# A hybrid attention and recurrence block: the opening stage rewritten around the second half of x

## The chip, the cores and the metric

The kernel runs on one core of a Trainium2 chip. The metric is the device time of one execution in microseconds (us), the median of several. The profile speaks of five engines: PE (TensorE, the matrix multiplications; PEld is its loading of the stationary operand), DVE (VectorE), ACT (ScalarE), POOL (GpSimd) and SP (SyncE, whose queue issues nearly all transfers of this kernel). Each engine works through its own queue in order.

## The reference

One layer of an encoder block on x of 1024 tokens by 1024 channels, all in float32:

```python
h = rms_norm(h_res, norm_w[layer])
z = jnp.einsum('bsd,dc->bsc', h, w_in[layer].astype(f32))
qkv_a, g_a, q_b, zf_fwd, zf_bwd, i_b, g_b, zgate_a, zgate_b = jnp.split(z, split_points, axis=-1)
...
merged = jax.nn.sigmoid(zgate_a) * y_a + jax.nn.sigmoid(zgate_b) * y_b
h_res = h_res + jnp.einsum('bsd,de->bse', merged, w_out[layer].astype(f32))
```

`rms_norm` divides each token's row by its root mean square and multiplies it by a weight per channel. Behind the one wide projection `z` come three groups of banded attention (8 heads of 64 each) and a gated linear recurrence in both directions. What matters here is only the start: the norm of x, and the first columns of `z`, which are the values V of the three attention groups (512 columns each).

## The kernel before, in words

**Numbers.** A float32 operand is split into a high part (a rounded type that PE takes at full speed, written by ACT) and a low part (what is left, a subtraction). Each product of two such operands is three matmuls: high by high, high by low, low by high. Weights are read in pages of 128x512 (`raw`), which become `whi` and `wlo`; x is normalised and split into `hh` and `hl` (in the code `hq[0]`, `hq[1]`, read through `hs`).

**Order.** The program is emitted by a planner. `Engine` and `Plan` (from line 46) keep a modelled clock for each engine; `Builder.tick` (line 251) puts a waiting task into its engine's queue once its inputs will be there within 1.4 us of PE's modelled clock. Each engine then runs its queue in order, and waits where the model was too early. Weight pages are split in order by such tasks after `b.auto()` (line 353), at most `RING` = 9 pages ahead of the last page that is freed; raw pages have 4 buffers. `run_unit` (line 484) runs one or several accumulation groups side by side over eight steps `kk`; a function `pre` may emit work ahead of each step. PSUM has two rings of tiles: `b.gps` with 3 and `b.bank` with 5. Finished groups are copied by ACT into one of 3 `stage` tiles and stored to DRAM through SP's queue.

**The opening** (lines 685 to 924). x comes transposed, `xT`, as 16 tiles of 128 channels x 512 tokens: half `k` = 0 holds tokens 64 to 575, half `k` = 1 tokens 576 to 1023 and 0 to 63.

1. The first half is multiplied by the norm's weights only (`prep_u`, line 710: `uhi` on ACT, `ulo` on DVE) and projected unnormalised into four PSUM tiles `ups` (loop at line 861), 8 x 4 x 3 = 96 matmuls. Beside it ACT squares x and DVE adds the squares into `acc`; the second half is squared in the loop's step 5 (`XB`). The low parts of the weights are made on POOL (`split`, line 358).
2. Within step 6 PE sums `acc` over the channels (`ss`, in `inv_rms`, line 722, for both halves at once), DVE makes the reciprocal root of the mean (`rsqrt`, line 553), and `spread` (line 731) turns it into a row on all partitions: DVE writes a diagonal `dg`, PE multiplies it with ones into `rB`.
3. The second half is normalised with `prep_h` (line 740: DVE x*w*rB, ACT `hh`, DVE `hl`), and `bias_tables` (line 772) writes the attention's bias tables to DRAM; each is then blown up there from DRAM to DRAM (`skewD<-tabD`).
4. Four groups of 128 tokens for V of attention group 0 run in two units: tokens 576 and 704, with `pre_b` normalising the second half step by step, then tokens 832 and the edge group (tokens 0 to 63 and 960 to 1023, whose operands POOL copies into `uhi`, `ulo` in `edge`). Meanwhile ACT scales the four `ups` with the reciprocal root into `stage` tiles (`scaled_v`), and the second unit's `pre_a` normalises the first half, which is loaded a second time through 4 buffers `x`.

**After it** (lines 926 to 992). V of attention groups 1 and 2: for each, six units of one group of 128 tokens and one unit of two, 8 x 24 matmuls. Beside them, for each of four blocks `c` of channels, `sums_h` on POOL and `sums_1`, `sums_2` on DVE form sums and differences of blocks of h, which `put_sum` splits (`S0h`, `S0l` ...). When all 16 are written (`blocks_start`), `run_quads` (line 432) starts with its products into `qA`: a scheme with 7 products for 8 in place of the plain projection. Then come attention, recurrence and output, which the change does not touch.

Of the kernel before, what the change touches and what calls it, by code (L numbers as in the profile page):

```python
# [18 lines left out]
S = 1024  # L19
# [10 lines left out]
LOWS = ("T2", "T4")  # L30
XR, SQ = 4, 2
XB = {5: (0, 1, 2, 3, 4, 5, 6, 7)}

# [177 lines left out]
class Builder:  # L211
# [145 lines left out]

    def split(self, raw, low="pool"):
        hi, lo = self.hir.get(), self.lor.get()
        scale = self.scales.get(self.split_next)  # L360
        if scale is None:
            self.p.act.activation(hi, raw, AF.Copy)
            getattr(self.p, low).tensor_tensor(lo, raw, hi.bitcast(F32), op=OP.subtract)
# [120 lines left out]
    def run_unit(self, unit):  # L484
# [87 lines left out]
def hybrid_block(ctx, tc, a, out):  # L572
# [114 lines left out]

    def load_x(k, d, new):
        xs[k, d] = new()
        s_.dma_start(xs[k, d], a["xT"][8 * k + d])  # L690

    def new_x():
        return pre.tile([128, 512], F32, tag="x", name=b.name("x"), bufs=XR)

    for d in range(4):
        load_x(0, d, new_x)
        b.feed()
    wp = bank("warm")
    for k in range(WARM):
# [10 lines left out]
    def prep_u(d):  # L710

        add = square(0, d - 1, xs[0, d - 1]) if d > 0 else None
        if d < 8:
            a_.activation(uhi[:, d], xs[0, d], AF.Copy, scale=nw[:, d:d + 1])
            v_.scalar_tensor_tensor(ulo[:, d], xs[0, d], nw[:, d:d + 1], uhi[:, d].bitcast(F32),
                                           op0=OP.mult, op1=OP.subtract)
        if d > 0:
            add()
            if d + XR - 1 < 8:
                load_x(0, d + XR - 1, new_x)  # L720

    def inv_rms():
        ps = b.gps.get(name="ss")
        for j in range(8):
            t_.matmul(ps[:, j:j + 1], acc[j // 4][:, 128 * (j % 4):128 * (j % 4) + 128], ones[:, 0:1],
                             start=True, stop=True)
        r = rsqrt(b, tiny, ps[:, 0:8], 8, 1.0 / D, "x")
        b.gps.done(ps)
        return r

    def spread(r):

        dg = pre.tile([128, 512], F32, tag="sq", name=b.name("dg"), bufs=SQ).rearrange("p (a t) -> p a t", a=4)
        v_.tensor_tensor(dg, ident[:, None, :].to_broadcast([128, 4, 128]),
                                r[:, :, None].to_broadcast([128, 4, 128]), op=OP.mult)
        ps = bank("rB")
        t_.matmul(ps, ones, dg, start=True, stop=True)
        return ps

    def prep_h(k, d, rB):  # L740

        parts = ((0, A0, 512 - A0), (512 - A0, 512, A0)) if k == 0 else ((0, A1, S - A1), (S - A1, 0, A0))
        if d < 8:
            x = xs[k, d]
            v_.scalar_tensor_tensor(x, x, nw[:, d:d + 1], rB, op0=OP.mult, op1=OP.mult)
            for c, t, n in parts:
                a_.activation(hs(0, d, t, n), x[:, c:c + n], AF.Copy)
        if d > 0:
# [14 lines left out]
    g_.memset(rb[32:33, :], NEG)  # L763
    oh = [stage.get() for _ in range(3)]

    def bias_rows():
        p = b.gps.get(name="tab")
        for g in range(3):
            t_.matmul(p[32 * g:32 * g + 8, 0:TABW], rb[:, 8 * g:8 * g + 8], oh[g][0:33, 0:TABW], start=True, stop=True)
        return p  # L770

    def bias_tables(p):
        g_.tensor_scalar(nqk[:, 0:3], nqk[:, 0:3], -0.125 / 128.0, None, op0=OP.mult)
        g_.tensor_scalar(nqk[:, 3:6], nqk[:, 3:6], -1.0 / 128.0, None, op0=OP.mult)
        for g in range(3):
            stage.done(oh[g])
            t = stage.get()
# [58 lines left out]

    def evac_v(g, t0, scale=None):
        def f(ps):
            t = stage.get()
            if scale is None:  # L840
                a_.activation(t, ps, AF.Copy)
                b.gps.done(ps)
            else:
                a_.activation(t, ps, AF.Copy, scale=scale)
            put[g] = put.get(g, 0) + 1
            if t0 < 0:
                def both():
                    s_.dma_start(vD[g, 0:64], t[0:64])
                    s_.dma_start(vD[g, S - 64:S], t[64:128])
                    stage.done(t)  # L850
                b.task("sp", [t], both, 1)
            else:
                store(vD[g, t0:t0 + 128], t)
        return f

    for d in range(LEAD):
        b.split_next_page()
        prep_u(d)
    ups = [bank("u") for _ in range(4)]
    rs = {}  # L860
    for d in range(8):
        wh, wl = b.w[d]
        for j in range(4):
            c = slice(128 * j, 128 * j + 128)
            for i, (l, r) in enumerate(((uhi[:, d, c], wh), (uhi[:, d, c], wl), (ulo[:, d, c], wh))):
                t_.matmul(ups[j], l, r, start=(d == 0 and i == 0), stop=(d == 7 and i == 2))
            if d == 6 and j == 1:
                r_ = inv_rms()
                for t in acc:
                    v_ring.done(t)  # L870
                for e in range(XR):
                    load_x(0, e, new_x)
        if d < 9 - LEAD:
            prep_u(d + LEAD)
            if d < 8 - LEAD:
                b.split_next_page()
        if d == 0:
            for e in range(8):
                load_x(1, e, v_ring.get)
            s_.dma_start(nqk, a["qk_w"])  # L880
            s_.dma_start(rb[0:32, :], a["rel_bias"])
            for g in range(3):
                s_.dma_start(oh[g][0:33, 0:TABW], a["c_onehot"][:, g])
        if d in XB:
            for e in XB[d]:
                square(1, e, xs[1, e])()
    rB = spread(r_[:, 4:8])
    groups = [tok_group(pos, t, evac_v(0, t), last=(t < 0 or t == 832),
                        first=(lambda d: (uhi[:, d, 0:128], ulo[:, d, 0:128])) if t < 0 else None)
              for t in (576, 704, 832, -64)]  # L890
    for d in range(2):
        prep_h(1, d, rB)
    bias_tables(bias_rows())
    b.auto()
    for j in range(4):
        b.task("act", [ups[j], r_], lambda j=j: scaled_v(j), 4, stage.soon, after=b.p.t["pe"] + 2.0 * j)

    def scaled_v(j):
        evac_v(0, 64 + 128 * j, r_[:, j:j + 1])(ups[j])

    def pre_b(kk):
        if kk < 7:
            prep_h(1, kk + 2, rB)
            edge(kk + 1)
        if kk == 0:
            edge(0)

    def edge(d):
        for e, u in enumerate((uhi, ulo)):
            for c, t in ((0, 0), (64, S - 64)):  # L910
                g_.tensor_copy(u[:, d, c:c + 64], hs(e, d, t, 64))

    def pre_a(kk):
        if kk == 0:
            rs["A"] = spread(r_[:, 0:4])
            prep_h(0, 0, rs["A"])
        prep_h(0, kk + 1, rs["A"])

    groups[0]["pre"] = pre_b
    groups[2]["pre"] = pre_a  # L920
    b.run_unit(groups[:2])
    b.run_unit(groups[2:])
    pos += 8
# [33 lines left out]
    def sums_2(c, x):  # L957
        v_.tensor_tensor(x[0, 1], x[0, 1], x[0, 0], op=OP.subtract)
        for k, t in ((0, x[1, 1]), (1, x[0, 0]), (2, x[2, 0]), (3, x[0, 1])):
            put_sum(k, c, t)  # L960

    for c in range(4):
        b.task("pool", [h[c2][:, c] for h in hq for c2 in h], lambda c=c: sums_h(c), 4, lambda: tmp.soon(5))

# [1071 lines left out]
```

## Time and profile before

| | us |
|---|---|
| median of 3 runs (1573.1 to 1578.47) | 1573.38 |
| the profiled execution's own time | 1571.46 |
| its span, from first to last instruction | 1569.7 |
| PE busy | 1517.6 |
| DVE busy | 960.9 |
| ACT busy | 807.4 |
| POOL busy | 481.3 |

The trace lists every instruction by its start and its duration. Matmuls overlap in the pipeline, so that a listed matmul of 0.39 us doesn't mean that the next starts 0.39 us later; the distance between starts is what counts. A name such as `gp<-whi,hh` gives the tile written and the tiles read (for PE the moving operand first). An entry in square brackets is the idle time ahead of an instruction and what ended it. PEclk is the share of full clock granted to PE. Nearly all instructions carry the line 56 of a helper, so tiles tell them apart.

### The profile page before, as it was taken

To read this page: it belongs to the slowest core of one execution; us is meant where nothing else is said; L and a number is where in the kernel's file an instruction comes from. 1 tells how busy PE (TensorE), PEld (TensorE's weight loads), DVE (VectorE), ACT (ScalarE), POOL (GpSimd) and SP (SyncE) were. 2 spreads that over 40 slices of the span, in tenths; PEclk is the share of its full clock that TensorE was granted. 3 is DMA by queue.
4 is the path that set the end of the run, shared out by engine and by line. 5 is a ranking of instruction groups with operands and counts; after the bars stand their busy time and mean duration, and the time that the engine had idled before them with its cause. 6 is when DMAs were issued, how large, how long until landed. Compare 5 with 4: busy or idle time off the path is not lost. (4 is left out here: it accounts for less than half of the span.)

```text
span 1569.7 us, 23099 instructions
## 1 busy us (share of the span) xinstructions
PE 1517.6 (97%) x8109; PEld 1238.1 (79%) x8109; DVE 960.9 (61%) x1891; ACT 807.4 (51%) x1693; POOL 481.3 (31%) x481
## 2 busy tenths in 40 slices
PE   8789999999999999999999999999999999999999
PEld 7578887778777787778777788878877878888887
DVE  6671487778878764544423438889788887643211
ACT  5523476666666655777642146565564642633210
POOL 3382333323333340020023254443243423003320
PEclk8999999999999999999999999999999999999999
DMA  7434433323425247465555651131211312842232
GB/s 220 138 104 131 132 101 120 119 71 118 116 56 141 67 141 245 148 193 152 151 149 157 208 165 41 48 101 41 86 50 41 103 40 74 307 123 94 87 122 93
DMA packets 171536, 188.15 MB, mean 120 GB/s; under 512 B 43297, under 2 KB 105884, under 8 KB 171420
## 3 DMA queue, kind: packets, MB, share of 16 engines
q1 hardware_dynamic: 163996, 186.23, 38.4%
q8 instruction: 64, 1.05, 0.3%
q10 hardware_dynamic: 7424, 0.45, 0.3%
q14 instruction: 52, 0.43, 0.1%
HBM read 130.69 MB, written 60.66 MB: 122 GB/s over the span
## 5 line engine op out<-in xcount | busy, mean ns | idle before, releaser
L56 POOL TENSOR_TENSOR wlo<-raw,whi 128x512 fp32r<-128x512 f32 x136 | 181.3, 1341 | 423.4 <-ACT whi L56 405.9
L56 POOL TENSOR_TENSOR wlo<-qraw,whi 128x512 fp32r<-128x512 f32 x100 | 137.4, 1380 | 296.3 <-ACT whi L56 266.8
L56 PE MATMUL gp<-whi,hh 128*128 128x512 f32 x344 | 142.4, 414 | 11.6 <-ACT hh L56 8.1
L56 ACT ACTIVATE whi<-raw 128x512 fp32r<-128x512 f32 x136 | 84.5, 626 | 111.0 <-PE gp L56 81.8
L56 PE MATMUL gp<-wlo,hh 128*128 128x512 f32 x344 | 137.7, 400 | 1.2 <-POOL wlo L56 1.1
L56 PE MATMUL gp<-hh,whi 128*128 128x512 f32 x336 | 137.9, 410 | 0.0
L56 PE MATMUL gp<-whi,hl 128*128 128x512 f32 x344 | 137.4, 399 | 0.5 <-DVE hl L56 0.5
L56 PE MATMUL gp<-hh,wlo 128*128 128x512 f32 x336 | 131.8, 392 | 0.0
L56 PE MATMUL gp<-hl,whi 128*128 128x512 f32 x336 | 131.4, 391 | 0.0
L56 ACT ACTIVATE whi<-qraw 128x512 fp32r<-128x512 f32 x140 | 85.9, 624 | 52.4 <-DVE qraw L56 35.2
L56 ACT ACTIVATE stage<-gp 128x512 f32<-128x512 f32 x60 | 35.3, 595 | 120.7 <-PE gp L56 103.1
L56 PEld LDWEIGHTS gp<-whi,hh 128*128 128x128 f32 x344 | 66.3, 193 | 34.4 <-ACT hh L56 9.3
L56 ACT ACTIVATE as<-as,neg 128x192 f32<-128x192 f32 (+2 forms) x192 | 83.7, 439 | 8.8 <-DVE neg L56 8.8
L56 DVE TENSOR_TENSOR qraw<-qraw,qraw 128x512 f32<-128x512 f32 x80 | 69.5, 870 | 29.0 <-POOL wlo L56 24.2
L56 PEld LDWEIGHTS gp<-whi,hl 128*128 128x128 f32 x344 | 66.4, 193 | 15.9 <-DVE hl L56 1.7
L56 PEld LDWEIGHTS gp<-wlo,hh 128*128 128x128 f32 x344 | 66.5, 193 | 15.6 <-POOL wlo L56 2.9
L56 DVE COPY apt<-pT 128x512 f32<-128x512 f32 (+2 forms) x50 | 29.0, 584 | 77.9 <-PE pT L56 77.9
L56 PE MATMUL gp<-sh,whi 128*128 128x512 f32 x192 | 74.7, 389 | 0.0
L56 PE MATMUL gp<-sl,whi 128*128 128x512 f32 x192 | 74.7, 389 | 0.0
L56 PE MATMUL gp<-sh,wlo 128*128 128x512 f32 x192 | 74.7, 389 | 0.0
L56 PEld LDWEIGHTS gp<-hh,wlo 128*128 128x128 f32 x336 | 63.4, 189 | 14.0
L56 PEld LDWEIGHTS gp<-hh,whi 128*128 128x128 f32 x336 | 63.7, 190 | 11.3
(255 smaller groups left out, 4042.9 us busy)
## 6 DMA issues: line engine op xcount, KB each, us to landing
raw<-in_w_in_dram SPq DMA_DIRECT2D x112, 256.0 KB, 2.8
qraw<-in_w_in_dram SPq DMA_DIRECT2D x80, 256.0 KB, 3.6
qkD<-ny SPq DMA_DIRECT2D x48, 256.0 KB
igD<-stage SPq DMA_DIRECT2D x32, 256.0 KB, 2.2
ig<-igD SPq DMA_DIRECT2D x32, 256.0 KB, 4.8
sgl<-sgD SPq DMA_DIRECT2D x32, 256.0 KB, 3.3
sgD<-stage SPq DMA_DIRECT2D x26, 256.0 KB, 2.2
ak<-qkD SPq DMA_DIRECT2D x6, 1024.0 KB, 7.3
```

The costliest lines, as they stand in the source:

```text
L56: got = f(*args, **kw)
```

## The change

- **Loads.** All eight tiles of the first half get tiles of their own, and are requested at the start: four beside the first weight pages, four right behind them. The second half is requested behind the first four splits instead of within the loop's step 0. The first half isn't loaded a second time. The one-hot matrix for the bias tables gets a tile of its own instead of the three `stage` tiles.
- **Low parts of the weights** are made on DVE instead of POOL while `b.low` is "dve", which is until the opening ends.
- **Squares.** The loop squares tiles 0 to 5 of the first half, then (in step 3) all eight of the second. PE's sum over channels is now for one half at a time: the second half's in step 7 of the loop, behind its first group. Tiles 6 and 7 of the first half are squared later, in steps 0 and 1 of the next unit, and its sum follows in step 3.
- **Unscaled products.** ACT copies the four `ups` unscaled into tiles `uv` (`keep_u`), scales them there when the root is known (`scaled_u`), and stores them from there.
- **One unit of four groups** (576, 704, 832 and the edge), the edge group in a `b.bank` tile. Its operands are read straight from the normalised x: POOL copies the high part, DVE subtracts.
- **The first half** is normalised by `pre_a` within the first three units of attention group 1 (one tile in three steps); these take the tokens in the order 640, 768, 896, and then 512, 0, 128 and so on. The last `prep_h(0, 8)`, which makes the low part of tile 7, is emitted twice.
- **Bias tables** are made behind the second of those units.
- **Sums.** `sums_h` runs on DVE instead of POOL, and each `put_sum` becomes a task of ACT of its own.

```diff
+    b.low = "dve"
     for d in range(4):
-        load_x(0, d, new_x)
+        load_x(0, d)
         b.feed()
+    for d in range(4, 8):
+        load_x(0, d)
...
     def prep_u(d):
-        add = square(0, d - 1, xs[0, d - 1]) if d > 0 else None
...
+        add = square(0, d - 1, xs[0, d - 1]) if 0 < d <= EA else None
...
-            if d == 6 and j == 1:
-                r_ = inv_rms()
...
+            if d == 7 and j == 0:
+                ss = b.gps.get(name="ss")
+                r1 = inv_rms(1, ss)
+                b.gps.done(ss)
...
+        if d == 3:
...
+            for e in range(8):
                 square(1, e, xs[1, e])()
...
+    rB = spread_out(spread(r1))
+    uv = [pre.tile([128, 512], F32, name=f"uv{j}") for j in range(4)]
+    groups = [tok_group(pos, t, evac_v(0, t), last=True) for t in (576, 704, 832)]
+    groups.append(tok_group(pos, -64, evac_v(0, -64, b.bank), last=True, first=lambda d: (uhi[:, d, 0:128], ulo[:, d, 0:128])))
+    groups[3]["ring"] = b.bank
...
+    def edge(d):
+
+        x = xs[1, d][:, 384:512]
+        g_.tensor_copy(uhi[:, d, 0:128], x)
+        v_.tensor_tensor(ulo[:, d, 0:128], x, uhi[:, d, 0:128].bitcast(F32), op=OP.subtract)
...
     def pre_b(kk):
+        if kk == 0:
+            edge(0)
         if kk < 7:
             prep_h(1, kk + 2, rB)
             edge(kk + 1)
...
+        if kk < 4:
+            keep_u(kk)
+        if EA + kk < 8:
+            square(0, EA + kk, xs[0, EA + kk])()
+        if kk == 8 - EA + 1:
+            rs["r"] = inv_rms(0, bank("ss"))
+            for j in range(4):
+                b.task("act", [rs["r"], uv[j]], lambda j=j: scaled_u(j), 4)
+
+        if kk == 5:
+            rs["dg"] = spread(rs["r"])
+        if kk == 7:
+            rs["A"] = spread_out(rs["dg"])
...
+    b.run_unit(groups)
...
+    def pre_a(kk):
+        if steps[0] % 3 == 0 and steps[0] < 27:
+            prep_h(0, steps[0] // 3, rs["A"])
+        steps[0] += 1
+
+    order = (5, 6, 7, 4, 0, 1, 2, 3)
+    grs = [tok_group(pos, 128 * i, evac_v(1, 128 * i), last=(k >= 6)) for k, i in enumerate(order)]
+    for k in range(3):
+        grs[k]["pre"] = pre_a
+        b.run_unit([grs[k]])
+        if k == 1:
+            bias_tables(bias_rows())
+    pre_a(0)
+    prep_h(0, 8, rs["A"])
...
     pctx.close()
+    b.low = "pool"
...
-            g_.tensor_tensor(x[t, k], hq[0][t, k][:, c].bitcast(F32), hq[1][t, k][:, c].bitcast(F32), op=OP.add)
+            v_.tensor_tensor(x[t, k], hq[0][t, k][:, c].bitcast(F32), hq[1][t, k][:, c].bitcast(F32), op=OP.add)
...
-            put_sum(k, c, t)
+            b.task("act", [t], lambda k=k, t=t: put_sum(k, c, t), 4)
```

More of the change, by code (lines that the diff above doesn't have):

```diff
@@ L30 @@
 LOWS = ("T2", "T4")
-XR, SQ = 4, 2
-XB = {5: (0, 1, 2, 3, 4, 5, 6, 7)}
+SQ, EA = 2, 6
 def _dram(ap, offset, dims):
@@ L217 @@
     eager = False
+    low = "pool"
     def __init__(self, ctx, tc, a):
@@ L356, in auto, with split @@
             self.offer(t, k)
-    def split(self, raw, low="pool"):
+    def split(self, raw, low=None):
         hi, lo = self.hir.get(), self.lor.get()
@@ L362, in split @@
             self.p.act.activation(hi, raw, AF.Copy)
-            getattr(self.p, low).tensor_tensor(lo, raw, hi.bitcast(F32), op=OP.subtract)
+            getattr(self.p, low or self.low).tensor_tensor(lo, raw, hi.bitcast(F32), op=OP.subtract)
         else:
@@ L686, in hybrid_block, with load_x @@
     xs = {}
-    def load_x(k, d, new):
-        xs[k, d] = new()
+    def load_x(k, d):
+        xs[k, d] = v_ring.get() if k else pre.tile([128, 512], F32, name=b.name("x"))
         s_.dma_start(xs[k, d], a["xT"][8 * k + d])
-    def new_x():
-        return pre.tile([128, 512], F32, tag="x", name=b.name("x"), bufs=XR)
+    b.low = "dve"
     for d in range(4):
-        load_x(0, d, new_x)
+        load_x(0, d)
         b.feed()
+    for d in range(4, 8):
+        load_x(0, d)
     wp = bank("warm")
@@ L710, in prep_u, with inv_rms @@
     def prep_u(d):
-        add = square(0, d - 1, xs[0, d - 1]) if d > 0 else None
[L713 to L717, printed above, removed]
-            add()
[L719 to L729, printed above, removed]
+        add = square(0, d - 1, xs[0, d - 1]) if 0 < d <= EA else None
+        a_.activation(uhi[:, d], xs[0, d], AF.Copy, scale=nw[:, d:d + 1])
+        v_.scalar_tensor_tensor(ulo[:, d], xs[0, d], nw[:, d:d + 1], uhi[:, d].bitcast(F32),
+                                       op0=OP.mult, op1=OP.subtract)
+        if add is not None:
+            add()
+    def inv_rms(k, ps):
+        for j in range(4):
+            t_.matmul(ps[:, j:j + 1], acc[k][:, 128 * j:128 * j + 128], ones[:, 0:1], start=True, stop=True)
+        return rsqrt(b, tiny, ps[:, 0:4], 4, 1.0 / D, "x")
     def spread(r):
@@ L735, in spread, with spread_out @@
                                 r[:, :, None].to_broadcast([128, 4, 128]), op=OP.mult)
+        return dg
+    def spread_out(dg):
         ps = bank("rB")
@@ L763, in hybrid_block @@
     g_.memset(rb[32:33, :], NEG)
-    oh = [stage.get() for _ in range(3)]
+    oh = pre.tile([33, 3, TABW], F32, name="oh")
     def bias_rows():
@@ L768, in bias_rows @@
         for g in range(3):
-            t_.matmul(p[32 * g:32 * g + 8, 0:TABW], rb[:, 8 * g:8 * g + 8], oh[g][0:33, 0:TABW], start=True, stop=True)
+            t_.matmul(p[32 * g:32 * g + 8, 0:TABW], rb[:, 8 * g:8 * g + 8], oh[:, g], start=True, stop=True)
         return p
@@ L775, in bias_tables @@
         for g in range(3):
-            stage.done(oh[g])
             t = stage.get()
@@ L835, in hybrid_block, with evac_v @@
     put = {}
-    def evac_v(g, t0, scale=None):
+    def evac_v(g, t0, ring=b.gps):
         def f(ps):
             t = stage.get()
[L840 to L844, printed above, removed]
+            a_.activation(t, ps, AF.Copy)
+            ring.done(ps)
             put[g] = put.get(g, 0) + 1
@@ L847, in both @@
                 def both():
-                    s_.dma_start(vD[g, 0:64], t[0:64])
-                    s_.dma_start(vD[g, S - 64:S], t[64:128])
+                    s_.dma_start(vD[g, S - 64:S], t[0:64])
+                    s_.dma_start(vD[g, 0:64], t[64:128])
                     stage.done(t)
@@ L858, in hybrid_block @@
         prep_u(d)
+    for e in range(8):
+        load_x(1, e)
     ups = [bank("u") for _ in range(4)]
-    rs = {}
     for d in range(8):
@@ L866, in hybrid_block @@
                 t_.matmul(ups[j], l, r, start=(d == 0 and i == 0), stop=(d == 7 and i == 2))
-            if d == 6 and j == 1:
-                r_ = inv_rms()
[L869 to L873, printed above, removed]
-            prep_u(d + LEAD)
[L875 to L879, printed above, removed]
+            if d == 7 and j == 0:
+                ss = b.gps.get(name="ss")
+                r1 = inv_rms(1, ss)
+                b.gps.done(ss)
@@ L880, in hybrid_block @@
+        if d + LEAD < 8:
+            b.split_next_page()
+            prep_u(d + LEAD)
+        if d == 3:
             s_.dma_start(nqk, a["qk_w"])
             s_.dma_start(rb[0:32, :], a["rel_bias"])
[L882 to L885, printed above, removed]
+            s_.dma_start(oh, a["c_onehot"])
+            for e in range(8):
                 square(1, e, xs[1, e])()
-    rB = spread(r_[:, 4:8])
@@ L888, in hybrid_block @@
-    groups = [tok_group(pos, t, evac_v(0, t), last=(t < 0 or t == 832),
-                        first=(lambda d: (uhi[:, d, 0:128], ulo[:, d, 0:128])) if t < 0 else None)
-              for t in (576, 704, 832, -64)]
+    rB = spread_out(spread(r1))
+    uv = [pre.tile([128, 512], F32, name=f"uv{j}") for j in range(4)]
+    groups = [tok_group(pos, t, evac_v(0, t), last=True) for t in (576, 704, 832)]
+    groups.append(tok_group(pos, -64, evac_v(0, -64, b.bank), last=True, first=lambda d: (uhi[:, d, 0:128], ulo[:, d, 0:128])))
@@ L891, in hybrid_block, with keep_u, scaled_u @@
+    groups[3]["ring"] = b.bank
+    b.auto()
     for d in range(2):
         prep_h(1, d, rB)
[L893 to L899, printed above, removed]
+    rs = {}
+    def keep_u(j):
+        a_.activation(uv[j], ups[j], AF.Copy)
+    def scaled_u(j):
+        a_.activation(uv[j], uv[j], AF.Copy, scale=rs["r"][:, j:j + 1])
+        b.task("sp", [uv[j]], lambda: (s_.dma_start(vD[0, 64 + 128 * j:192 + 128 * j], uv[j]), rs.__setitem__(j, 1)), 1)
@@ L904, in pre_b @@
             edge(kk + 1)
[L905 to L911, printed above, removed]
-    def pre_a(kk):
[L914 to L923, printed above, removed]
+        if kk < 4:
[4 more added lines that the diff above has]
+            rs["r"] = inv_rms(0, bank("ss"))
+            for j in range(4):
+                b.task("act", [rs["r"], uv[j]], lambda j=j: scaled_u(j), 4)
[3 more added lines that the diff above has]
+            rs["A"] = spread_out(rs["dg"])
+    groups[0]["pre"] = pre_b
+    keep_u(0)
+    keep_u = lambda j, f=keep_u: f(j) if j else None
+    b.run_unit(groups)
+    pos += 8
+    put[0] = 8
+    steps = [0]
+    def pre_a(kk):
+        if steps[0] % 3 == 0 and steps[0] < 27:
[10 more added lines that the diff above has]
+    prep_h(0, 8, rs["A"])
+    b.until(lambda: all(j in rs for j in range(4)))
     pctx.close()
+    b.low = "pool"
     gctx, sctx, tctx = ExitStack(), ExitStack(), ExitStack()
@@ L959, in sums_2 @@
         for k, t in ((0, x[1, 1]), (1, x[0, 0]), (2, x[2, 0]), (3, x[0, 1])):
-            put_sum(k, c, t)
+            b.task("act", [t], lambda k=k, t=t: put_sum(k, c, t), 4)
     for c in range(4):
-        b.task("pool", [h[c2][:, c] for h in hq for c2 in h], lambda c=c: sums_h(c), 4, lambda: tmp.soon(5))
+        b.task("dve", [h[c2][:, c] for h in hq for c2 in h], lambda c=c: sums_h(c), 4, lambda: tmp.soon(5))
     def blocks_start():
@@ L981, in blocks_start @@
         b.start_quads(blk["raw"])
-    for g, order in ((1, range(8)), (2, (4, 5, 6, 7, 0, 1, 2, 3))):
-        grs = [tok_group(pos, 128 * i, evac_v(g, 128 * i), last=(k >= 6)) for k, i in enumerate(order)]
+    for g in (1, 2):
+        if g == 2:
+            grs = [tok_group(pos, 128 * i, evac_v(g, 128 * i), last=(k >= 6))
+                   for k, i in enumerate((4, 5, 6, 7, 0, 1, 2, 3))]
         for k, gr in enumerate(grs[:6]):
+            if g == 1 and k < 3:
+                continue
             b.run_unit([gr])
```

6 lines of the change are left out of this document (1 added, 5 removed).

## Prediction, made before the changed kernel was run

> **What bounds the kernel now.** I read the page first, then the chain that ended last, the waits of PE up to 165 us, the stages by windows, and the timeline of the opening.
>
> ```profile
> span 1569.7 us, 23099 instructions
> ...
> PE 1517.6 (97%) x8109; PEld 1238.1 (79%) x8109; DVE 960.9 (61%) x1891; ACT 807.4 (51%) x1693; POOL 481.3 (31%) x481
> ```
> ```profile
> 1336.11 229.88 PE gp L56 x1014
> ```
> ```profile
> PE gp L56 <- ACT hh L56: 8.1, 2, 7.4
> PE ss L56 <- DVE v L56: 4.4, 1, 4.4
> PE gp L56 <- ACT stage L56: 2.8, 1, 2.8
> ```
> ```profile
> 6.50:25.10 18.60, 18.41 (x80) 14.41 (x79) 15.11 (x16) 13.93 (x25) 9.71 (x7) 1.00 0.88 288
> 25.10:41.20 16.10, 11.08 (x42) 8.16 (x42) 8.64 (x21) 4.34 (x8) 0.96 (x2) 0.68 0.40 127
> 171.10:1569.70 1398.60, 1365.73 (x7484) 1117.11 (x7482) 872.74 (x1765) 738.72 (x1563) 407.97 (x397) 1.00 0.38 116
> ```
>
> PE is busy for 97% of the span, and the chain of the end is PE work for its last 230 us. The windows give the length, then busy time (and instructions) of PE, PEld, DVE, ACT, POOL, then PE's granted clock, the DMA share and GB/s. Behind 171.10 PE is 98% busy at full clock; in 25.10 to 41.20 it is 69% busy at a clock of 0.68. So time that PE doesn't lose ahead of 171 us moves the end by as much. These are the borders of that stretch:
>
> ```profile
> 6.53 0.48 PE L56 MATMUL u<-whi,uhi 128*128 128x512 f32 x1
> ...
> 41.25 0.50 PE L56 MATMUL gp<-whi,hh 128*128 128x512 f32 x1 [0.70 <-ACT hh L56]
> ...
> 74.87 0.39 PE L56 MATMUL gp<-whi,hh 128*128 128x512 f32 x1
> ...
> 84.56 0.61 PE L56 MATMUL gp<-whi,hh 128*128 128x512 f32 x1
> ...
> 112.04 0.39 PE L56 MATMUL gp<-whi,hh 128*128 128x512 f32 x1
> ...
> 127.61 0.39 PE L56 MATMUL gp<-whi,hh 128*128 128x512 f32 x1
> ...
> 170.90 0.39 PE L56 MATMUL gp<-whi,hl 128*128 128x512 f32 x1
> ```
>
> These are the first `u` product and, counted through the timeline, numbers 1, 97, 121, 241, 289 and 480 of the `gp` products. From 127.61 to 170.90 lie 191 steps, 0.2266 us each: PE's dense pace. Against it the opening (96 products, 21.8 us) takes 34.7 and loses 12.9; the two units of V of group 0 (96) take 33.6 and lose 11.8; the first unit of group 1 (24) loses 4.3; the five after it (120) 0.3; the last pair (48) 4.7; group 2 nothing. Together 34.0 us: no more than this is to be had.
>
> **The opening part by part.**
>
> ```profile
> 7.55 0.63 ACT L56 ACTIVATE whi<-raw 128x512 fp32r<-128x512 f32 x1 [1.93 <-DMA raw<-in_w_in_dram]
> ...
> 21.26 0.68 DVE L56 TENSOR_TENSOR v<-v,sq 128x512 f32<-128x512 f32 x1
> 21.86 1.78 DVE L56 SCALAR_TENSOR_TENSOR ulo<-x,nw,uhi 128x512 fp32r<-128x512 f32 x1
> 23.57 6.89 DVE L56 TENSOR_TENSOR v<-v,sq 128x512 f32<-128x512 f32 x9
> 25.10 1.05 PE L56 MATMUL ss<-ones,v 128*128 128x1 f32 x8
> 30.52 1.86 PE L56 MATMUL ss<-ones,v 128*128 128x1 f32 x8 [4.36 <-DVE v L56]
> 32.42 0.17 DVE L56 TENSOR_SCALAR rv<-ss 128x8 f32<-128x8 f32 x1 [1.96 <-PE ss L56]
> 34.63 0.69 DVE L56 TENSOR_TENSOR dg<-ident,rr 128x512 f32<-128x512 f32 x1
> 38.78 1.02 PE L56 MATMUL rB<-dg,ones 128*128 128x512 f32 x2
> ...
> 39.73 0.82 PE L56 MATMUL tab<-stage,rb 33*8 33x384 f32 x6
> ```
>
> PE reached `ss` at 25.10 with 78 products done, 0.9 later than its pace gives from 6.53. With 87 ahead of it, it comes there at 27.1. When is the second half's sum ready? Loads go at 288 GB/s (first window), 0.91 us for 256 KB. The fourth was there by 7.55, so the thirteenth, weight page 4, which now follows four x tiles, comes at about 15.7; PE wants it at 18.3. From there DVE does low part, `ulo` and an addition for each of three pages and two operations for the last, 11 in all. They took 0.68 (21.26) and up to 1.78 (21.86) beside POOL's low parts. POOL makes none now, so I take 0.7: 7.7 us, to 24.0 with ACT's 0.6 ahead. Seven additions for the second half at 0.77 (6.89 for nine) end at 29.4. I take 28.8, a little less, since the window's mean rate holds the queue's gaps too; 27.1, no wait at all, is the lower bound. A wait of 1.7 remains of the 4.36. Then `ss` (four columns, 1.05), root (32.42 to 34.63, 2.2), `dg` 0.69 and hops of 0.4 put `rB` at 33.15; the last nine `u` products (2.0) fit into that, where before 18 of them at lowered clock held `rB` back from 35.3 to 38.78. From `rB` to the first `gp` 2.47 as before; the table's matmuls in that gap (39.73) were hidden by the wait on `hh`, and go. First `gp` at 35.6 in place of 41.25: **5.6 gained**; 7.3 are still lost.
>
> **The four groups.**
>
> ```profile
> 43.92 0.73 SPq L56 DMA_DIRECT2D skewD<-tabD  x1
> ...
> 45.87 2.40 SPq L56 DMA_DIRECT2D vD<-stage  x3
> ...
> 55.69 0.69 ACT L56 ACTIVATE stage<-u,rr 128x512 f32<-128x512 f32 x1 [8.08 <-DMA vD<-stage]
> ...
> 56.90 0.80 PE L56 MATMUL gp<-whi,hh 128*128 128x512 f32 x1 [7.45 <-ACT hh L56]
> ```
> ```profile
> L56 DVE TENSOR_TENSOR hl<-v,hh 128x448 fp32r<-128x448 f32 x8 | 5.9, 734 | 7.9 <-ACT hh L56 7.9
> L56 DVE SCALAR_TENSOR_TENSOR v<-v,nw,rB 128x512 f32<-128x512 f32 x8 | 5.8, 739 | 4.5 <-PE rB L56 4.5
> L56 DVE TENSOR_TENSOR hl<-v,hh 128x64 fp32r<-128x64 f32 x8 | 2.0, 244 | 0.0
> ```
>
> Here the fourth scaled copy waited for a `stage` tile whose store sat behind the blown-up table: 45.87 to 55.69. ACT runs in order, so `hh` stood behind it, and PE behind `hh`: 7.45. The copies into `uv` need no such tile and the table comes later, so this wait goes. What is late next is DVE. Over the unit it does eight times 0.74 + 0.73 + 0.24 for the second half, eight low parts at 0.68, eight `edge` subtractions (128x128, not in the trace: between 0.24 for 64 columns and 0.73 for 448; 0.3), two additions, the root and `dg`: 13.7 + 5.4 + 2.4 + 1.4 + 2.9 = 25.8, less the overlap of neighbouring operations (rows start 0.67 apart). PE has 21.8 + 1.05 (`ss`) + 1.02 (`rA`) = 23.9. They nearly tie; I give PE 1.0 for the first two steps, where DVE starts with it. POOL's copies, ACT's `uv` copies and squares run ahead and cost nothing unless DVE's queue stops for them; if it did, each is under 0.7. The wait of `rsqrt` on `ss` in step 3 holds DVE for 2.2 us, and behind it stands the `hl` of step 5, two steps off, so PE feels nothing.
>
> ```profile
> 26.00:27.00 1.00, 0.15 (x2) 1.00 0.32 61
> 27.00:28.00 1.00, 0.00 (x0) 0.50 0.88 305
> 33.00:34.00 1.00, 1.00 (x4) 0.50 0.11 41
> ```
>
> Clock (after the busy time of PE): PE stopped at 26.15 and the clock halved at 27.0, with only one-column `ss` products in the two us before. At 33 four products fit in a us. The changed kernel has three gaps of 1.2 to 1.7 us within 9 us, with `ss` and `rB` between; one lowered stretch while PE has work (some 4 us at half pace) costs 2.0, and none or two are the bounds, 0 and 4. The Trainium skill, "TensorE: Matmul & The Clock Gate", Part 1, has the clock fall after an idle window of about 3.4 us; by that rule no gap here is long enough, and the sum would be 2.0 less. The row speaks against it, since PE had been idle for under 1 us.
>
> So the unit takes 23.9 + 1.0 + 2.0 = 26.9 for 21.8: 5.1 lost instead of 11.8, **6.7 gained**, and ends at 62.5.
>
> **Groups 1 and 2.**
>
> ```profile
> 79.79 0.50 PE L56 MATMUL gp<-wlo,hh 128*128 128x512 f32 x1 [0.86 <-POOL wlo L56]
> ...
> 113.47 0.63 ACT L56 ACTIVATE S1h<-xs 128x512 fp32r<-128x512 f32 x1 [2.77 <-DVE xs L56]
> ...
> 115.67 0.75 PE L56 MATMUL gp<-whi,hh 128*128 128x512 f32 x1 [2.79 <-ACT stage L56]
> ...
> 122.16 0.69 DVE L56 TENSOR_TENSOR S3l<-xs,S3h 128x512 fp32r<-128x512 f32 x1
> ```
>
> In the first unit of group 1, PE ate pages faster than POOL made low parts. Pages 8 to 15 now become free to split one per step of the four-group unit (2.7 us, against DVE's 0.7), so all are ready: **4.3 gained**. In the pair, PE waited for an evacuation that stood on ACT behind `S1h`, which waited for DVE. With `put_sum` a task of its own, and DVE alone on the sums (48 operations at 0.69, 33 us), this mostly goes. Bounds for it are 0 and the old 4.7; I keep 1.5, nearer to none since an evacuation has two units (10.9 us) to spare. The table's matmuls (0.82) now stand on PE's path and are added. Normalising the first half (1.7 a tile, three steps or 2.0 us each) hides under PE; the doubled `hl`, 1.0, does too. Gain here 4.3 + 0.3 + 4.7 - 1.5 - 0.8 = **7.0**.
>
> **Sum:** 5.6 + 6.7 + 7.0 = 19.3. The profiled execution took 1571.5 (1.8 around its span), so 1552.2; the median of the runs lies 1.9 above that execution, so **1554.1**, said as 1554.
>
> **The rivals.**
>
> *DVE sets the opening's pace.* For it: 25.8 against 23.9 in the unit, and a sum of squares that may come 0.6 later. Against: operations start closer than they last. Price 1.9 + 0.6, and a second lowered clock stretch 2.0: 4.5, so 1558.6.
>
> *The store wait comes back in groups 1 and 2.* The tables now fall into units that also store through three `stage` tiles. For it: 9.8 us behind one table. Against: a tile comes round after three units, 16.3 us. It decides if two tables follow within 16 us. Price 7.45 and 2.0 of clock: 1563.5.
>
> *Slower: the sums hold up the products of* `qA`. Those need all 16 parts, ready at 122.85 before, with 48 us to spare. On DVE the 48 operations at 1.78 (beside POOL's low parts) take 85.4 us; they start at 79.6 (62.5, three units, 0.8), so end at 165. Loads, a split and a low part follow, which took the opening 6.5 from nothing to its first product: `qA` at 171.5, and 2.0 of clock, where before it followed the last `gp` at 171.1. That is 2.4 slower: 1575.8. It decides from DVE's end at 162.6 on. The Trainium skill, "SBUF — State Buffer", Who interferes with whom, has DVE operations with two SBUF inputs shut out for the whole of a POOL read; by that rule each can pay. Only some 8 low parts fall into this stretch, so I hold it unlikely.
>
> *No effect:* the start of `qA` hangs on something that doesn't move, a transfer for instance. Nothing in the waits names one: 1573.
>
> **How the numbers follow.** About 0.5% (7.9 us) is what a measurement of this kernel can tell from none. Chances: forecast 0.60, DVE 0.20, store wait 0.12, no effect 0.05, slower 0.03. All of the first three lie below 1565.5, but the third nearly at it: faster 0.90; same 0.08; slower 0.02, the far end of the last. The range takes the forecast's bounds (clock 2.0, pair 1.5, squares 1.4 less: 1549; one more for pages and hops) and the first two rivals up to the store wait: 1548 to 1564.
>
> **What would show it.** In the profile after: `ss` waits under 3 us on DVE's `v`; first `gp` near 35.6; no wait of ACT on `vD<-stage` ahead of the unit's end at 62.5; no PE wait on `wlo` in group 1; none on `stage` over 1.5; `qA` from 152. Wrong if the first `gp` comes after 39, if ACT waits on a store in groups 1 and 2, or if `qA` starts after 160.

## The result, and the profile after

| | before | after |
|---|---|---|
| median of 4 runs each, us | 1575.47 (1573.1 to 1578.47) | 1551.97 (1546.83 to 1554.76) |
| the profiled execution's own time | 1571.46 | 1546.83 |
| its span | 1569.7 | 1545.0 |

The ratio of after to before is 0.9846, with a 95% interval of 0.9812 to 0.988: 1.5% faster, 23.5 us. The forecast was 1554 within 1548 to 1564.

The page of the changed kernel, its waits of PE up to 165 us, and its stages by windows (length, busy time and instructions of PE, PEld, DVE, ACT, POOL, then granted clock, DMA share, GB/s):

```profile
span 1545.0 us, 23058 instructions
...
PE 1508.1 (98%) x8109; PEld 1232.0 (80%) x8109; DVE 966.8 (63%) x1945; ACT 809.7 (52%) x1697; POOL 435.4 (28%) x424
```
```profile
PE gp L55 <- ACT hh L55: 1.4, 1, 1.4
PE warm L55 <- DVE warm L55: 1.4, 1, 1.4
PE gp L55 <- DVE hl L55: 1.2, 1, 1.2
PE rB L55 <- DVE dg L55: 0.9, 1, 0.9
PE ss L55 <- DVE v L55: 0.3, 1, 0.3
```
```profile
33.60:59.70 26.10, 24.69 (x106) 19.01 (x107) 20.49 (x53) 16.51 (x36) 4.71 (x9) 1.00 0.35 113
59.70:104.20 44.50, 44.50 (x199) 36.07 (x198) 39.35 (x64) 22.19 (x47) 7.52 (x5) 1.00 0.42 142
104.20:147.70 43.50, 43.50 (x193) 36.02 (x192) 14.82 (x18) 13.12 (x22) 10.43 (x8) 1.00 0.37 115
147.70:1545.00 1397.30, 1365.84 (x7484) 1117.39 (x7483) 869.43 (x1765) 738.77 (x1563) 411.89 (x397) 1.00 0.38 117
```

No wait of PE in this stretch is longer than 1.45 us; before there was one of 7.4, one of 4.4 and one of 2.8. PE has as many instructions as before (8109). From 59.70 on it is busy throughout, in the stage in which DVE now has the most to do (39.35 of 44.50). Behind `qA` the two kernels need nearly the same: 1397.3 here from 147.70, 1398.6 before from 171.10. So the gain lies in front of `qA`, at the borders that the prediction used (timeline of the changed kernel):

```profile
6.07 0.48 PE L55 MATMUL u<-whi,uhi 128*128 128x512 f32 x1
...
27.03 1.02 PE L55 MATMUL ss<-ones,v 128*128 128x1 f32 x8 [0.27 <-DVE v L55]
...
31.10 1.10 PE L55 MATMUL rB<-dg,ones 128*128 128x512 f32 x2 [0.89 <-DVE dg L55]
...
33.65 0.50 PE L55 MATMUL gp<-whi,hh 128*128 128x512 f32 x1 [1.45 <-ACT hh L55]
...
59.73 0.39 PE L55 MATMUL gp<-whi,hh 128*128 128x512 f32 x1
...
65.17 0.39 PE L55 MATMUL gp<-whi,hh 128*128 128x512 f32 x1
...
104.23 0.39 PE L55 MATMUL gp<-whi,hh 128*128 128x512 f32 x1
...
147.75 0.39 PE L55 MATMUL qA<-hh,whi 128*128 128x512 f32 x1
```

The first `u` is 0.5 us earlier than before; the opening up to the first `gp` takes 27.6 in place of 34.7, the four groups 26.1 in place of 33.6, the first unit of group 1 5.4 in place of 9.7, the rest of group 1 39.1 in place of 43.1, group 2 its 43.5 as before. Together `qA` starts 23.4 us earlier (171.13 before).

### The profile page after: what moved, and what is told of

Read it like the earlier page. It is cut to its first block, busy times and chain, and to the rows that moved or that the text cites. A ratio compares the mean times of both kernels' runs of the same rounds, so it can differ in the third digit from the quotient of the medians.

```text
span 1545.0 us, 23058 instructions
## 1 busy us (share of the span) xinstructions
PE 1508.1 (98%) x8109; PEld 1232.0 (80%) x8109; DVE 966.8 (63%) x1945; ACT 809.7 (52%) x1697; POOL 435.4 (28%) x424
## 5 line engine op out<-in xcount | busy, mean ns | idle before, releaser
L55 POOL TENSOR_TENSOR wlo<-raw,whi 128x512 fp32r<-128x512 f32 x119 | 161.3, 1361 | 437.1 <-ACT whi L55 424.1
L55 POOL TENSOR_TENSOR wlo<-qraw,whi 128x512 fp32r<-128x512 f32 x100 | 141.2, 1420 | 289.7 <-ACT whi L55 260.6
L55 PEld LDWEIGHTS gp<-hh,whi 128*128 128x128 f32 x336 | 63.7, 190 | 11.3
```

Source lines behind the costliest of these rows:

```text
L55: got = f(*args, **kw)
```

## The experiments

The total of one kernel varies by 3 to 14 us between runs, so parts of a few us can't be told apart by it. The borders in the trace are sharper: in the six other runs that leave the opening as changed, the first `gp` came 26.7 to 28.2 us after the first `u`, in the changed kernel 27.6. But each border comes from one profile, so a difference under 1.5 us at a border isn't shown by it alone. Each experiment has both, in us. `gp` 97 is the first product of attention group 1, 121 that of its second unit, 289 that of group 2. Each ratio is to runs of the kernel before that were taken beside it (their medians lie between 1572.26 and 1575.47), so ratios compare better than medians:

| kernel | first `u` | first `gp` | `gp` 97 | `gp` 121 | `gp` 289 | `qA` | median | ratio to before, 95% |
|---|---|---|---|---|---|---|---|---|
| before | 6.53 | 41.25 | 74.87 | 84.56 | 127.61 | 171.13 | | |
| after | 6.07 | 33.65 | 59.73 | 65.17 | 104.23 | 147.75 | 1551.97 | 0.9846 (0.9812, 0.9880) |
| after, once more | 6.55 | 34.02 | 61.20 | 66.64 | 105.70 | 149.22 | 1549.87 | 0.9848 (0.9824, 0.9873) |
| before, late table | 6.54 | 41.18 | 67.72 | 75.48 | 113.59 | 164.11 | 1564.83 | 0.9938 (0.9917, 0.9958) |
| before, new sums | 6.55 | 40.88 | 74.80 | 86.08 | 125.43 | 168.95 | 1572.94 | 0.9999 (0.9981, 1.0017) |
| before, both | 6.32 | 40.72 | 67.62 | 76.59 | 114.71 | 158.23 | 1560.99 | 0.9920 (0.9903, 0.9937) |
| after, old sums | 5.68 | 33.52 | 59.60 | 65.04 | 109.14 | 162.44 | 1562.60 | 0.9937 (0.9909, 0.9965) |
| after, sums on POOL | 6.01 | 34.24 | 60.32 | 65.76 | 109.79 | 161.36 | 1563.42 | 0.9930 (0.9906, 0.9955) |
| after, `put_sum` direct | 6.02 | 33.34 | 59.46 | 64.90 | 103.96 | 148.50 | 1552.22 | 0.9859 (0.9833, 0.9884) |
| after, two units | 6.38 | 33.06 | 64.15 | 69.59 | 108.65 | 152.17 | 1554.27 | 0.9867 (0.9833, 0.9900) |
| after, low parts on POOL | 6.20 | 35.30 | 60.82 | 66.26 | 105.32 | 148.84 | 1554.53 | 0.9870 (0.9837, 0.9904) |
| after, all squares first | 6.55 | 34.45 | 60.92 | 66.36 | 105.42 | 148.94 | 1551.65 | 0.9859 (0.9838, 0.9880) |
| after, late root | 6.19 | 33.44 | 59.82 | 65.71 | 104.77 | 148.29 | 1551.81 | 0.9861 (0.9837, 0.9884) |
| after, late root and filled gaps | 5.66 | 32.99 | 58.43 | 64.32 | 103.38 | 146.90 | 1548.33 | 0.9843 (0.9824, 0.9861) |

**The late table, alone.** In the kernel before, the bias tables move behind the second unit.

```diff
-    oh = [stage.get() for _ in range(3)]
+    oh = pre.tile([33, 3, TABW], F32, name="oh")
...
-    bias_tables(bias_rows())
     b.auto()
...
     b.run_unit(groups[2:])
+    bias_tables(bias_rows())
```

> The kernel before with one part of the change alone: the bias tables are made behind the second unit of group 0 (their one-hot matrix in a tile of its own). Theory (the store wait behind the blown-up table costs 7.45 us of PE and 2.0 of clock behind it): 7 to 9.5 us less than before, ratio 0.994 to 0.9955, and no wait of ACT on vD<-stage ahead of 63 us. Rival (the wait is only the last of several that end together, and DVE or the pages take its place): under 3 us less, ratio above 0.998.

The ratio is 0.9938, 9.5 us, the upper end of what the theory gave; in the profile the two units of group 0 gain 7.1 (26.5 for 33.6). The trace shows more. Up to product 289, where group 2 starts, the gain is 14.0 us. The pair, too, loses nothing now (10.9 from 102.71 to 113.59), though the sums are as before. But 7.0 of the 14.0 are lost in group 2, which had lost nothing before:

```profile
116.60 0.50 PE L56 MATMUL gp<-whi,hh 128*128 128x512 f32 x1 [1.49 <-ACT whi L56]
...
118.11 0.50 PE L56 MATMUL gp<-wlo,hh 128*128 128x512 f32 x1 [1.00 <-POOL wlo L56]
...
119.79 0.80 PE L56 MATMUL gp<-wlo,hh 128*128 128x512 f32 x1 [0.72 <-POOL wlo L56]
```

PE now comes to group 2's pages before ACT and POOL have made them.

**The sums as before, in the changed kernel.**

```diff
-            v_.tensor_tensor(x[t, k], hq[0][t, k][:, c].bitcast(F32), hq[1][t, k][:, c].bitcast(F32), op=OP.add)
+            g_.tensor_tensor(x[t, k], hq[0][t, k][:, c].bitcast(F32), hq[1][t, k][:, c].bitcast(F32), op=OP.add)
...
-            b.task("act", [t], lambda k=k, t=t: put_sum(k, c, t), 4)
+            put_sum(k, c, t)
...
-        b.task("dve", [h[c2][:, c] for h in hq for c2 in h], lambda c=c: sums_h(c), 4, lambda: tmp.soon(5))
+        b.task("pool", [h[c2][:, c] for h in hq for c2 in h], lambda c=c: sums_h(c), 4, lambda: tmp.soon(5))
```

> The changed kernel with the sums as before: sums_h on POOL, put_sum called directly. Theory (the pair of group 1 lost 4.7 us because its evacuation stood behind put_sum on ACT): 3 to 5 us more than the changed kernel, so some 18 us less than before (0.9885), with a PE wait on ACT stage of 2 to 3 us in the pair. Rival (the sums start some 7 us earlier now, and an evacuation has 10.9 us to spare, so their form costs nothing): within 1 us of the changed kernel, 0.986.

`qA` starts 14.7 us later than in the changed kernel, where I expected 3 to 5, and the ratio is 0.9937 for the changed kernel's 0.9846 and 0.9848. The timeline of the pair and of group 2's start, with what stopped each engine:

```profile
95.26 0.63 ACT L55 ACTIVATE S1h<-xs 128x512 fp32r<-128x512 f32 x1 [1.80 <-DVE xs L55]
...
96.83 0.57 ACT L55 ACTIVATE stage<-gp 128x512 f32<-128x512 f32 x1
...
97.46 0.80 PE L55 MATMUL gp<-whi,hh 128*128 128x512 f32 x1 [3.40 <-ACT stage L55]
```
```profile
111.90 0.50 PE L55 MATMUL gp<-wlo,hh 128*128 128x512 f32 x1 [1.70 <-POOL wlo L55]
...
114.11 0.63 ACT L55 ACTIVATE S1h<-xs 128x512 fp32r<-128x512 f32 x1 [2.72 <-DVE xs L55]
116.35 0.79 PE L55 MATMUL gp<-whi,hh 128*128 128x512 f32 x1 [1.87 <-ACT whi L55]
```
```profile
109.10:162.40 53.30, 48.28 (x193) 37.53 (x193) 13.73 (x14) 15.34 (x26) 17.64 (x13) 0.90 0.33 104
```

The pair loses its 5.0 as expected (104.23 less 93.35 there, 109.14 less 93.22 here). Group 2 loses 9.8 more: its low parts and its high parts stand on POOL and on ACT behind the sums, and with these waits the clock is 0.90 on the mean of the stage, the last row.

**Which half of that change?** Two runs, each with one half of the diff above: the sums on POOL with `put_sum` still a task of its own, and the sums on DVE with `put_sum` called directly.

> The changed kernel with sums_h on POOL again, but each put_sum still a task of its own. Theory (two separate causes: POOL's sums stand ahead of group 2's low parts, which cost 9.8 us at group 2's start, and put_sum called directly stands ahead of the pair's evacuation, 5.0 us): waits on wlo at the start of group 2 stay, the pair's wait goes, and qA starts near 157.5. Rival (both come from ACT standing behind put_sum): qA near 148.

> The changed kernel with put_sum called directly as before, but sums_h on DVE. By the theory of two causes: the pair's wait on ACT stage comes back with up to 5.0 us, no wait on wlo, qA between 150 and 153. Rival (the direct call costs something only where DVE waits for POOL's sums): qA at 147.8 to 148.5.

The theory of two causes fell. With POOL's sums the pair's wait came back in spite of the tasks (3.4), and group 2 lost 8.0, most of the 9.8 with the old sums; `qA` at 161.36. With the direct call alone `qA` starts at 148.50, 0.75 later, and group 2 takes 44.5 for 43.5, with one wait of 0.71 on POOL's `wlo`. So it is the engine for all but some 1 us. The groups of the stage show how, first of the changed kernel, then with the old sums (count, busy time, mean ns):

```profile
L55 DVE TENSOR_TENSOR xs<-xs,xs 128x512 f32<-128x512 f32 x16 | 11.8, 755 | 0.3
L55 DVE TENSOR_TENSOR xs<-hh,hl 128x512 f32<-128x512 f32 x16 | 14.4, 959 | 0.1
```
```profile
L55 DVE TENSOR_TENSOR xs<-xs,xs 128x512 f32<-128x512 f32 x16 | 21.1, 1340 | 4.7 <-POOL xs L55 4.1
L55 POOL TENSOR_TENSOR xs<-hh,hl 128x512 f32<-128x512 f32 x16 | 25.3, 1608 | 30.3 <-DVE hl L55 22.3 <-DVE S0l L55 6.7 <-DVE S2l L55 0.6
```

Sixteen additions take 14.4 us on DVE and 25.3 on POOL, and beside POOL DVE's own take 1340 ns in place of 755. A likely link, read from the code and not tested: the planner sets DVE's 512 columns down at 0.61 us and POOL's at 1.24, so it thought the sums done sooner than they were, and put `S1h` ahead of the evacuation and of the pages in ACT's queue, as a task or not.

**The new sums in the kernel before, and both parts in it.**

> The kernel before with the change of the sums alone: sums_h on DVE, each put_sum a task of its own. The last two runs put the whole cost on POOL's sums. Then here only the pair of group 1 gains, since its group 2 loses nothing: 4.7 us, qA at 166.4, ratio 0.997. Rival (DVE has no room for 16 more operations, or the wait in the pair has another cause): qA at 171 or later.

> The kernel before with two parts: late bias tables and the new sums. The late tables alone brought 14.0 us up to the first product of group 2 and kept 7.0 of them at qA, with waits on wlo in between. Theory (the other 7.0 went back because POOL's sums came ahead of group 2's low parts): no wait on wlo, qA near 157, ratio 0.991. Rival (POOL's low parts themselves are too slow there): qA stays near 164.

Alone the sums bring nothing that can be measured in the total (0.9999, interval 0.9981 to 1.0017, where I expected 0.997), and `qA` at 168.95 lies between the theory's 166.4 and the rival's 171. The pair's 4.7 are gained (10.9 from 114.55 to 125.43), but the first unit of group 1 loses 1.6 (11.3 for 9.7), where POOL's low parts now run beside DVE's sums (five in 8.35 us from 78.34 on, in 6.21 before), and 1.0 goes in the units after it. With the late table together, group 2 has no wait on `wlo` any more (43.5 from 114.71 to 158.23) and `qA` starts at 158.23: 12.9 of the 23.4 us. The 7.0 that the late table had to give back are kept.

**Two units in place of one.**

```diff
-    groups = [tok_group(pos, t, evac_v(0, t), last=True) for t in (576, 704, 832)]
+    groups = [tok_group(pos, t, evac_v(0, t), last=(t == 832)) for t in (576, 704, 832)]
...
-    b.run_unit(groups)
+    b.run_unit(groups[:2])
+    b.run_unit(groups[2:])
```

> The changed kernel with the four groups in two units of two, as before. Theory (DVE needs about 2.4 us a step for the second half whatever PE does, and only four groups side by side give PE as much): the first unit runs at DVE's pace, some 20 us for 10.9 of PE work, the second at PE's, so 7 to 9 us more than the changed kernel, some 14 us less than before (0.991). Rival (the gain comes from the moved table and squares alone, and the number of units doesn't matter): within 1.5 us of the changed kernel, 0.986.

The first unit took 20.2 us (33.06 to 53.27) and the second 10.9: 31.1 for 26.1. The 20 us are the theory's number, but not by DVE's pace alone: PE waited for DVE 3.2 us in the first unit (0.38, 0.74 and 2.03), and the clock fell twice in it, to 0.83 on the mean:

```profile
33.00:53.20 20.20, 16.99 (x58) 12.19 (x59) 16.00 (x46) 11.52 (x28) 4.71 (x9) 0.83 0.19 65
```

`qA` comes 4.4 later than in the changed kernel, with that lowered clock in it: less than the 7 to 9 expected, where I had left out what the single unit itself loses (26.1 for 21.8). The totals don't tell the two apart (0.9867, interval 0.9833 to 0.9900).

**The low parts on POOL again**, without the line `b.low = "dve"`.

> The changed kernel with the weights' low parts of the opening on POOL again. Theory (a DVE operation beside a POOL low part takes 1.78 in place of 0.7 us, and the sum of squares and the four-group unit hang on DVE): the second half's squares end 3 to 5 us later and PE waits for them, 3 to 7 us more than the changed kernel, 0.988 to 0.9905. Rival (DVE sheds 17 operations of 0.69 us, which outweighs the slower ones): equal or up to 2 us less than the changed kernel, 0.985.

PE waited 1.54 for the squares (0.27 in the changed kernel), and the first `gp` came 1.65 later; by `qA` 1.1 of it was left. The direction at the first `gp` is the theory's, the size at most half of it. At `qA` nothing is shown: the unaltered kernel's second profile below starts it later still (149.22), and the ratio, 0.9870, is not told apart either.

**All squares of the first half first.**

```diff
-SQ, EA = 2, 6
+SQ, EA = 2, 8
...
+            square(0, 7, xs[0, 7])()
             for e in range(8):
                 square(1, e, xs[1, e])()
...
-        if kk == 8 - EA + 1:
+        if kk == 3:
```

> The changed kernel with all eight squares of the first half ahead of the second half's, two more on ACT and DVE. Theory (DVE's chain of additions ends just as PE arrives at ss): PE waits 1.6 to 2.0 us for it in place of 0.3, the first gp comes at 35.3 and the clock may fall: qA 1.5 to 3 us later than the changed kernel's 147.8 to 149.2. Rival (DVE has room there): first gp at 33.6 to 34.0.

PE waited 1.13 for `ss`, but counted from the first `u` the first `gp` came only 0.3 to 0.4 later (27.9 against 27.6 and 27.5). That lies between theory and rival, and within what the border varies by itself: the two deferred squares are at most a small part.

**The changed kernel once more.**

> The changed kernel once more, unaltered, beside the next three. If the three gaps of the opening (0.9 to 1.5 us) are too short to lower the clock, the profile shows full clock up to 148 us again and qA starts at 147.8 within 0.3; if the first profile was luck, the clock falls near 30 us and qA starts 1 to 3 us later. Ratio to before 0.986.

The first profile was luck in part. This time the clock fell (busy time of PE, clock, DMA share, GB/s by the microsecond):

```profile
31.00:32.00 1.00, 0.53 (x2) 1.00 0.00 0
32.00:33.00 1.00, 0.57 (x2) 1.00 0.00 0
33.00:34.00 1.00, 0.00 (x0) 1.00 0.00 0
34.00:35.00 1.00, 0.98 (x3) 0.64 0.00 0
35.00:36.00 1.00, 1.00 (x4) 0.50 0.00 0
36.00:37.00 1.00, 1.00 (x4) 0.50 0.00 0
37.00:38.00 1.00, 1.00 (x5) 0.65 0.00 0
```

It stood at half for some 3 us while PE had work, and `gp` 1 to 97 took 27.2 in place of 26.1.

**The root later, and the gaps filled.** The first half's sum and root move from step 3 to step 6 of the four-group unit; then also three idle matmuls ahead of `rB` and five behind it, on zeros, into tiles that are overwritten (the diff shows the late root).

```diff
-        if kk == 8 - EA + 1:
+        if kk == 6:
             rs["r"] = inv_rms(0, bank("ss"))
...
-        if kk == 5:
+        if kk == 7:
             rs["dg"] = spread(rs["r"])
-        if kk == 7:
-            rs["A"] = spread_out(rs["dg"])
...
+        if steps[0] == 0:
+            rs["A"] = spread_out(rs["dg"])
```

> The changed kernel with the first half's sum and root moved from step 3 of the four-group unit to step 6, behind the last hl (the diagonal to step 7, rA to the start of group 1). Theory (the 11 small operations hold DVE for 2 us in step 3, and PE waited 1.25 us for the hl behind them): that wait goes and qA starts at 146.5. Rival (DVE is simply full in this unit, so any 2 us of it are missed somewhere): another wait of about 1 us appears by the unit's end and qA starts at 147.5 or later. The total is expected 1 us under the changed kernel, which these rounds can't tell.

> The changed kernel with the late root and 8 idle matmuls (128x128 of zeros, results overwritten) in the gaps ahead of and behind rB. Theory (the clock falls in some runs because PE is idle for 0.9 and 1.5 us there; a filled gap keeps it up): full clock up to qA, which starts at 146.8 within 0.4. Rival (the fall is set by the one-column ss products or by chance): the clock falls near 30 us again and qA starts at 148 or later. The total would be 1 to 2 us under the changed kernel, too little to tell with these rounds.

With the late root the wait on `hl` fell from 1.25 to 0.47, at another step; the four groups, from which `rA` (1.0) has moved to the next unit, took 26.4 with the clock lowered once, and `qA` started at 148.29: 0.9 ahead of the repeat, whose clock fell too, and 0.5 behind the first profile, whose clock didn't. So the expectation for `qA` isn't settled by it. With the gaps filled the clock stayed full up to `qA`, at 146.90, where I had expected it, though 0.4 of that is an earlier start (first `u` at 5.66, in the changed kernel 6.07):

```profile
30.41 1.12 PE L55 MATMUL rB<-dg,ones 128*128 128x512 f32 x2
31.38 1.28 PE L55 MATMUL gp<-warm 128*128 128x128 f32 x10
32.99 0.50 PE L55 MATMUL gp<-whi,hh 128*128 128x512 f32 x1 [0.34 <-ACT hh L55]
```

One profile doesn't show that the filling did it. Of the seven profiles with this opening and its gaps unfilled, the clock stayed full there in four (the first, old sums, sums on POOL, `put_sum` direct) and fell in three (the repeat, two units, late root). Its median is the lowest of all, 1548.33, but its interval (0.9824 to 0.9861) covers the changed kernel's ratio.

## Why the prediction was right, and where its steps were off

**What bounds the kernel.** Right. Time that PE didn't lose ahead of `qA` came off the end: 23.4 at `qA`, 24.7 in the spans, 23.5 in the medians. That these agree so closely is partly luck, since the stretch behind `qA`, which no run edits, took 1397.3 to 1404.7 us in the fourteen profiles. The rivals "no effect" and "store wait" fell with this: ACT's waits on `vD<-stage` up to 125 us are 1.4 in total. Of the rival "DVE sets the opening's pace", priced at 4.5, what shows is PE's 0.27 on `v` and 1.25 on `hl`.

**The total: 19.3 forecast; 23.4 measured at `qA` in the first profile, 21.9 in the repeat.** All three parts came out larger than forecast. The median, 1551.97 for 1554, looks closer than that, in part because the kernel before's own median rose from 1573.38 to 1575.47 with its fourth run. Of the signs that were named, the waits are as forecast (none of PE on `wlo` in group 1 or on `stage`; ACT's on `vD<-stage` ahead of the unit's end is 0.4), and the two starts came earlier: the first `gp` at 33.65 for 35.6, `qA` at 147.75 for 152.

**The opening: 5.6 forecast; 7.6 at the first `gp`, 0.5 of them from the earlier start.** The step that was off is the thirteenth load, put at 15.7 us; it was there by 13.36, and the sum of squares was done at 26.9 in place of 28.8:

```profile
13.36 0.63 ACT L55 ACTIVATE whi<-raw 128x512 fp32r<-128x512 f32 x1 [1.00 <-DMA raw<-in_w_in_dram]
...
21.42 5.46 DVE L55 TENSOR_TENSOR v<-v,sq 128x512 f32<-128x512 f32 x7
```

So PE waited 0.27 and not 1.7. The first window's 288 GB/s was too low a rate: the kernel before requested many of those transfers one by one, and the changed kernel, which requests more of them in a row, moved 345 GB/s from 4.0 to 13.4. (The range's "squares 1.4 less" should be 1.7 by the prediction's own 28.8 and 27.1; 1548 holds with either.) The other half of this gain, as forecast, is that the root is no longer held back: from `ss` to `rB` 4.1 us in place of 8.3.

**The four groups: 6.7 forecast, 7.5 measured.** The store wait is right (first experiment). Two terms were wrong and partly cancelled. The clock, 2.0 for some 4 us at half pace, cost nothing in the first profile and some 1.1 in the second, with some 3 us lowered. And "PE feels nothing" of the root in step 3 was wrong, by 1.25:

```profile
46.99 0.15 DVE L55 TENSOR_SCALAR rv<-ss 128x4 f32<-128x4 f32 x1
...
49.03 0.69 DVE L55 TENSOR_TENSOR wlo<-raw,whi 128x512 fp32r<-128x512 f32 x1
49.64 0.74 DVE L55 SCALAR_TENSOR_TENSOR v<-v,nw,rB 128x512 f32<-128x512 f32 x1
50.30 0.85 DVE L55 TENSOR_TENSOR hl<-v,hh 128x448 fp32r<-128x448 f32 x2
...
50.98 0.50 PE L55 MATMUL gp<-whi,hl 128*128 128x512 f32 x1 [1.25 <-DVE hl L55]
```

The root waited in DVE's queue from 43.1, when `ss` was done, to 46.99; then came its 2.0, a low part and the normalising of the next tile, and only then the `hl` that PE stood waiting for. I had reckoned two steps of slack; DVE was already late by most of it, as the near tie of 25.8 against 23.9 should have told me. With the root moved, the longest wait on `hl` was 0.47.

**Groups 1 and 2: 7.0 forecast, 8.2 measured.** The pages of group 1 were ready (5.4 for 24 products), and the pair lost nothing, where I kept 1.5. Of the two reasons that I gave together, `put_sum` as a task of its own and DVE alone on the sums, the runs show 0.75 at `qA` for the first and 13.6 for the second. And I valued both at the pair's 4.7 alone. In the schedule of before they are worth little (2.2 at `qA`, nothing in the median); once the late table and the faster opening bring PE to group 2 earlier, leaving them as they were costs 14.7. The sum of the parts measured in before (7.0 and 2.2 at `qA`) is less than both together (12.9); in the totals (0.6%, nothing, 0.8%) this lies within the intervals. The prediction missed this new bound. That it was right on the total all the same is luck in this point: the change moves that bound out of the way.

**The slower rival** asked whether DVE's sums would hold up `qA`. They ended at 114.5, 33 us ahead of it. Its price of 1.78 an operation was met only where POOL made low parts at the same time; four additions took 2.50 us without POOL and 6.88 beside it:

```profile
83.69 2.50 DVE L55 TENSOR_TENSOR xs<-hh,hl 128x512 f32<-128x512 f32 x4
...
97.98 10.28 POOL L55 TENSOR_TENSOR wlo<-raw,whi 128x512 fp32r<-128x512 f32 x6 [0.55 <-ACT whi L55]
...
101.92 6.88 DVE L55 TENSOR_TENSOR xs<-hh,hl 128x512 f32<-128x512 f32 x4
```

The Trainium skill, "SBUF — State Buffer", Who interferes with whom, lets a DVE operation with two SBUF inputs and a POOL read shut each other out; the trace agrees in these rows and in those of the sums (1340 ns against 755), and the rule told against the kernel before, where both engines made the sums, more than against this one.

**What stays open** is when the clock falls. It did in the repeat, with gaps of 0.84 and 1.45 us around `rB`, and not in the first profile, with 0.89 and 1.45; over the seven profiles the gaps are the same within 0.05 us, so their length doesn't decide it. The Trainium skill, "TensorE: Matmul & The Clock Gate", Part 1, has it fall behind an idle window of about 3.4 us; the repeat doesn't agree, for PE was idle for at most 1.45 us at a time. Open, too, is most of the spread of the totals. Of the changed kernel's first four runs the one with a mean clock of 0.997 had a span of 1545.0, those with 0.993 and 0.994 had 1549.5 to 1552.9. But the fall near 34 us is the small part of it: of the 6.5 us between the spans of the first profile and the repeat, 1.5 arise up to `qA` and 5.0 behind it, where the clock was 0.99 for 1.00 and PE busy for 5.0 us longer:

```profile
149.20:1551.50 1402.30, 1370.86 (x7484) 1120.69 (x7482) 870.20 (x1765) 739.06 (x1563) 411.96 (x397) 0.99 0.38 117
```

Nor is it all longer matmuls: with `put_sum` direct that stretch took 1402.7, 5.4 more than in the first profile, and PE was busy for only 2.6 of them (1368.41). Nothing here shows what sets it.

## What to carry to other kernels

A part of a change is worth what it is worth in the schedule that the other parts make: time each in both, alone in the old kernel and undone in the new one, and read off at a border in the trace how much of a gain is still there further on. Where a wait goes, ask what the engine will now reach too early, and follow the queues in order, since an engine that is off the path still holds up everything behind the instruction on which it waits. Price two engines that share a resource by their rows side by side, not by each one's row alone.

## What the runs showed of the hardware that I had not expected

PE's granted clock halved after pauses as short as 0.84 and 1.45 us with a one-microsecond matmul between them, in one profile of the same kernel and not in the other. DVE and POOL slowed each other when both added or subtracted: sixteen 128x512 additions on POOL beside DVE took 1608 ns each, and DVE's own sixteen went from 755 on the mean to 1340. Four DVE additions in a row took 2.50 us without POOL and 6.88 beside its low parts, and five of POOL's low parts 8.35 us beside DVE's additions, 6.21 before.
